# A hybrid SSD and GLA trunk on one core: the first gate stage's last sixteen moving pieces are split in their own tiles, some sums come sooner, and a pair of gate matmuls moves

## The chip, the cores and the metric

The kernel runs on one core of a Trainium2 chip. The metric is the device time of one execution in microseconds (us). Five engines work side by side and meet only at semaphores: TensorE (PE) multiplies, VectorE (DVE), ScalarE (ACT) and GpSimd (POOL) work element by element, and SyncE (SP) issues most of the DMA transfers; ACT issues the stores of results. Each engine takes its instructions in a fixed order, so that an instruction that waits holds everything behind it on its engine.

## What is computed

One layer over 2048 tokens and 16 meta tokens in front of them, width 1024, all in float32. Two branches, a Mamba-2 scan (SSD) and gated linear attention (GLA, 4 heads), read one combined projection; their results are projected, weighted by sigmoid gates, summed and projected out:

```python
u = rmsnorm(hres, norm_w)
proj = jnp.einsum('bld,dn->bln', u, w_in)
z, xbc, dt_raw, q, k, v, g_gla, a_lr, merge_g = split_cols(proj, IN_WIDTHS)
...
gate_logit = jnp.einsum('blr,rk->blk', a_lr, gla_gate_w2) + gla_gate_b
log_a = (jax.nn.log_sigmoid(gate_logit.astype(jnp.float32)) / GLA_GATE_TEMP)
...
o = rmsnorm(jnp.concatenate([o_m, o_r], axis=1), gla_norm_w)
y_gla = o.reshape(b, l, GLA_DV) * jax.nn.silu(g_gla)
branches = jnp.stack([y_ssd.astype(y_gla.dtype), y_gla], axis=2)
branch_proj = jnp.einsum('blnc,ncd->blnd', branches, w_branch)
gates = jax.nn.sigmoid(merge_g.reshape(b, l, N_BRANCH, D_MODEL))
merged = jnp.sum(gates * branch_proj, axis=2)
return hres + jnp.einsum('bld,de->ble', merged, w_out)
```

## The kernel before

Every float32 factor is held as a high and a low part, and a product is three matmuls: `accum` (L212) issues high by high (L214), high by low (L215) and low by high (L216). So each piece that is multiplied is first split: ACT copies it to the high part, which rounds it, and DVE subtracts that from the piece, which gives the low part (POOL does it for some weights, L190).

The program has two halves. The first, to about 1458 us, goes through four blocks of 512 tokens (the first with the 16 meta tokens). For each it projects `u` by the columns of `w_in` (L214 to L216 with "ue" and "whl"), runs the SSD scan (L600 to L702) and the GLA scan (around L925 to L980). The pieces are generators which `step` advances in turn; PE's and SP's order in this half is the order in which the code issues (`manual_schedule`). `gates` makes the decay of the GLA heads, two heads in one turn: per head a matmul pair by the small gate weights `w2` (L488, into a bank "pj" for the segment with the meta tokens and a bank "pt" for the rest), read by DVE (L490) and ACT (L491); after both heads exp and ln on ACT (L493, L494), and the running sums later. In block 0 this falls between the z projections, which write the same two "pj" banks, and the SSD step that has L664, L689, L690 and L692 on PE. The z halves have 48 matmuls each.

In the second half (`Stage`, L1088) seven large multiplications (gates 0, two branches, gates 1, two branches, out) are done by a scheme of seven products over 2 by 2 blocks. A stage goes through rows n of blocks; each row has products p in the order 1, 2, 6, 7, 5, 3, 4, for two rows in turn. Each product is 4 pieces times 3 matmuls, 24 for a pair of rows. `b` are the moving pieces, 4 for each p: for p=1, 2 the blocks themselves, for 7, 5, 4 and 6 sums that were stored before, for p=3 a block. `load_b` (SP, L1103) brings a piece into a buffer "br", and `prep_b` splits it into a tile `b` (ACT L1108, DVE L1109). `a` are the stationary pieces: `load_a` loads four blocks a11, a21, a22, a12 of a row ("ar", L1115), `sum_a` makes on POOL s1 = a21 + a22 (L1124), s2 = s1 - a11 (L1125), a11 - a21 in place (L1126) and s4 = a12 - s2 (L1127), and `prep_a` splits what a product uses (ACT L1133, DVE L1134): a11 for p=1, a12 for 2, s2 for 6, a11 - a21 for 7, s1 for 5, s4 for 3, a22 for 4. `snapshot` (ACT L1168) keeps a partial sum, `total` (DVE L1185) adds one, and the gates take a tanh (ACT L1192) and are stored (L1382).

The first products of gates 0 (p = 1, 2, 6 of rows 0 and 1) are put between the steps of block 3's last GLA head, by the table `between`. That head ends with a mean of squares over each token (`ssq`), its inverse root `rstd` (DVE L258, then a power on POOL, L259), the scaling of the output "ot" (ACT L969), eight transposes on PE (L976), a product with the gate (DVE L977) and the store of y (L980). From there on only SP's order is written out by a table `todo`: `at(pos, fn)` puts a call behind the product number `pos`. A scheduler orders the other engines by these calls. The last sixteen moving pieces of the first stage are those of p = 7, 5, 3 and 4.

```python
pos = begins[si] - 12 + 0.8 * q if si else {3: -0.5, 4: 5.5, 5: 6.5, 6: 8.5}[q // 4]
at(pos - (4 if si else 0.1), lambda st=st, p=p, j=j: st.load_b(p, j))
at(pos, lambda st=st, p=p, j=j: st.prep_b(p, j))
```

Of the kernel before, what the change touches and what calls it, by code (L numbers as in the profile page):

```python
# [15 lines left out]
P = 128  # L16
# [27 lines left out]
def trunk_kernel(ctx: ExitStack, tc: tile.TileContext, xm, xmt, w_feat, w_tok, w_v3, w_zm, w_br, w_o,  # L44
# [423 lines left out]
    def gates(o):  # L468
# [12 lines left out]
        for h2 in range(0, GH, 2):  # L481
            gmt = mk(wk, [P, 2, META + BLK], F32, "tok4", bufs=NT4)
            for h in (h2, h2 + 1):
                gm = gmt[:, h % 2, :tt]
                gb = gate_b[:, h:h + 1]
                for i, (a, n) in enumerate(o.segs_all):
                    ps = bank(*((pj, "pj") if m0 and i == 0 else (pt, "pt")))
                    nc.tensor.matmul(ps[:, :n], w2[:, h * P:(h + 1) * P], ast[:, a:a + n],  # L488
                                     start=True, stop=True)
                    nc.vector.tensor_scalar(gm[:, a:a + n], ps[:, :n], gb, 0.0, op0=ALU.add, op1=ALU.min)  # L490
                    evicted[:] = [nc.scalar.activation(g_all[:, h, a:a + n], ps[:, :n], AF.Abs, bias=gb)]  # L491
            ga = g_all[:, h2:h2 + 2, :tt]
            nc.scalar.activation(ga, ga, AF.Exp, scale=-1.0)  # L493
# [294 lines left out]
    def gla_scan(o, h, last=False):  # L788
# [165 lines left out]
        for c0 in range(0, NCH, 2):  # L954
# [11 lines left out]
            yield  # L966
        r = rstd_of(ssq, 4, 1.0 / 256)
        for c in range(NCH):
            nc.scalar.activation(ot[:, c], ot[:, c], AF.Identity, scale=r[:, c:c + 1])  # L969
        yield  # L970
# [54 lines left out]

    early_b = {}

# [60 lines left out]
    class Stage:  # L1088
# [8 lines left out]
        def load_b(self, p, j):  # L1097
            src = {1: lambda j: self.braw(j, 0), 2: lambda j: self.braw(4 + j, 0), 3: lambda j: self.braw(4 + j, 1),
                   4: lambda j: self.sums[1][j][:, 1], 5: lambda j: self.sums[0][j][:, 1],
                   6: lambda j: self.sums[1][j][:, 0], 7: lambda j: self.sums[0][j][:, 0]}[p]  # L1100
            pool, tag, nb = bt_raws["early" if "all" not in bt_raws or (4 * PS.index(p) + j) % 3 == 2 else "all"]
            raw = self.braws[p, j] = mk(pool, [P, BLK], F32, tag, bufs=nb)
            nc.sync.dma_start(raw, src(j))  # L1103

        def prep_b(self, p, j):
            raw = self.braws[p, j]
            t = u_tile(0)[:, :, :BLK] if p < 3 else mk(bpl[p], [P, 2, BLK], F32R, f"b{p}")
# [13 lines left out]
        def sum_a(self, n):  # L1121
# [6 lines left out]
            self.a[n].update({3: s4, 4: a22, 5: s1, 6: s2, 7: a21})  # L1128

        def prep_a(self, n, p):  # L1130
            src = self.a[n][p]
            t = mk(apl, [P, 2, 4, P], F32R, "a")
            nc.scalar.activation(t[:, 0], src, AF.Copy)  # L1133
            latest[:] = [nc.vector.tensor_tensor(t[:, 1], src, t[:, 0].bitcast(F32), op=ALU.subtract)]  # L1134
            self.a[n][p] = t
# [213 lines left out]
    for si, st in enumerate(stages):  # L1349
        for q in range(0 if si else 12, 28):  # L1350
            p, j = PS[q // 4], q % 4
            pos = begins[si] - 12 + 0.8 * q if si else {3: -0.5, 4: 5.5, 5: 6.5, 6: 8.5}[q // 4]
            at(pos - (4 if si else 0.1), lambda st=st, p=p, j=j: st.load_b(p, j))
            at(pos, lambda st=st, p=p, j=j: st.prep_b(p, j))
# [31 lines left out]
    st.b.update(early_b)  # L1386

    def b_ops(j):
        st.load_b(6, j)
        st.prep_b(6, j)  # L1390

    def early(n, p):
# [6 lines left out]
        1: [],  # L1399
        2: [lambda: st.prep_a(0, 1), lambda: st.prep_a(1, 1)],  # L1400
        3: [lambda: early(0, 1), lambda: st.prep_a(0, 2)],
        4: [lambda: st.sum_a(0), lambda: early(1, 1), lambda: st.prep_a(1, 2)],
        5: [lambda: early(0, 2), lambda: st.prep_b(6, 0), lambda: st.load_b(6, 2)],
        6: [lambda: early(1, 2), lambda: st.sum_a(1), lambda: st.prep_b(6, 1), lambda: st.load_b(6, 3)],
        7: [lambda: st.prep_a(0, 6), lambda: st.prep_b(6, 2)],
# [121 lines left out]
```

## Time and profile before

| | |
|---|---|
| median of 3 runs | 2242.24 us (2240.61 to 2245.01) |
| the profiled execution | 2246.45 us |
| its span, first to last instruction | 2244.7 us |
| mean granted clock of TensorE | 0.997 |
| PE idle, all | 32.8 us |
| of it, waits for low halves of moving pieces (L1109) | 3.9 us, 3 times |
| of it, wait of the gate matmul (L488) | 3.1 us, once |

The profile is of one execution. In a timeline each row has the start and the length in us, the engine, the line, the operation, the tile written and those read, how many alike stand together, and in brackets how long the engine sat idle before it and what ended that. Lengths of matmuls overlap, since they are pipelined: the distance between starts tells what one costs. In a table of windows the columns are the window, its length, the busy time of PE, PE's weight loads, DVE, ACT and POOL with the number of instructions, the granted clock of PE, the busy share of the DMA engines, and GB/s. A row of the waits has what waited for what, total, times and longest. A row of DMA issues has KB of each and the median time from issue to landing.

### The profile page before, as it was taken

The page shows a single profiled execution, that of the slowest core. Times are in us where ns is not written, and L with a number is a line of the kernel's source. Part 1 is how long each engine was busy: PE and PEld are TensorE (multiplying, and loading weights), DVE is VectorE, ACT ScalarE, POOL GpSimd, SP SyncE. Part 2 cuts the span into 40 slices and gives each one's busy share as a digit, 9 for nine tenths or more (in the row PEclk, how much of TensorE's full clock was granted, in tenths as well). Part 3 has the DMA queues.
Part 4 walks back from the last instruction along what each step waited for, and adds up shares of the span by engine and source line. Part 5 has one row for each costly group of instructions (what it writes and reads, how often), then busy time and mean ns, then how long its engine had stood idle before and what let it go on. Part 6 is the DMA issues. An engine that isn't in the chain of part 4 may idle for free.

```text
span 2244.7 us, 34971 instructions
## 1 busy us (share of the span) xinstructions
PE 2211.9 (99%) x11789; PEld 1896.8 (85%) x11789; DVE 1577.0 (70%) x2935; ACT 1187.0 (53%) x2767; POOL 693.9 (31%) x689
## 2 busy tenths in 40 slices
PE   7999999999999999999999999999999999999998
PEld 7999999888888888888988888878888888888887
DVE  5775676677557676567677666674679945789866
ACT  5666655575445456544465544454644545454544
POOL 5444433223212122221212100066233374324341
PEclk9999999999999999999999999999999999999999
DMA  9767875767777667778667664376768866787753
GB/s 313 247 222 234 273 259 202 237 209 240 240 244 260 212 213 237 241 245 272 207 212 233 213 211 160 127 250 198 241 227 289 303 221 217 237 282 245 261 177 121
DMA packets 313699, 517.95 MB, mean 231 GB/s; under 512 B 28080, under 2 KB 162480, under 8 KB 313520
## 3 DMA queue, kind: packets, MB, share of 16 engines
q1 hardware_dynamic: 247008, 419.89, 57.8%
q10 hardware_dynamic: 65872, 93.74, 11.5%
q8 instruction: 92, 1.51, 0.3%
q0 software_dynamic: 640, 2.10, 0.2%
q14 instruction: 87, 0.71, 0.1%
HBM read 368.42 MB, written 147.19 MB: 230 GB/s over the span
## 4 chain that ended last, share of the span: by engine, by line
PE 89%; DVE 4%; DMA 3%; ACT 2%; issue 1%; POOL 1%; SPq 0%; POOLq 0%; ACTq 0%; DVEq 0%
PE pj L214 20%; PE pj L216 20%; PE pj L215 19%; PE pt L215 4%; PE pt L214 4%; PE pt L216 4%; PE pc L689 2%; PE pc L214 2%; PE pc L216 2%; PE pc L215 2%; PE pc L850 2%; PE pc L690 1%; DMA acc<-in_xmt 1%; PE pc L692 1%; PE pc L958 1%
## 5 line engine op out<-in xcount | busy, mean ns | idle before, releaser
L214 PE MATMUL pj<-ue,whl 128*128 128x264 f32 (+1 forms) x672 | 235.3, 350 | 1.9 <-ACT acc L596 1.2
L216 PE MATMUL pj<-ue,whl 128*128 128x264 f32 (+1 forms) x672 | 229.7, 342 | 0.0
L215 PE MATMUL pj<-ue,whl 128*128 128x264 f32 (+1 forms) x672 | 228.8, 340 | 0.0
L214 PE MATMUL pj<-uo,whl 128*128 128x512 f32 x512 | 205.7, 402 | 0.0
L216 PE MATMUL pj<-uo,whl 128*128 128x512 f32 x512 | 200.1, 391 | 0.0
L215 PE MATMUL pj<-uo,whl 128*128 128x512 f32 x512 | 199.5, 390 | 0.0
L214 PE MATMUL pj<-b,a 128*128 128x512 f32 (+1 forms) x484 | 188.9, 391 | 0.7 <-DVE io L1252 0.5
L216 PE MATMUL pj<-b,a 128*128 128x512 f32 (+1 forms) x484 | 188.9, 390 | 0.3 <-DVE a L1134 0.3
L215 PE MATMUL pj<-b,a 128*128 128x512 f32 (+1 forms) x484 | 187.6, 388 | 0.0
L600 DVE SCALAR_TENSOR_TENSOR acc<-cin,hcw,acc 128x512 f32<-128x512 f32 (+1 forms) x192 | 156.7, 816 | 39.7 <-ACT acc L596 38.6
L83 POOL TENSOR_TENSOR wr<-wr 128x256 f32<-128x256 f32 x80 | 66.0, 826 | 371.8 <-DMA wr<-y 158.1
L1124 POOL TENSOR_TENSOR as<-ar,ar 128x512 f32<-128x512 f32 x40 | 62.9, 1572 | 374.7 <-DMA ar<-in_w_br 179.9
L1134 DVE TENSOR_TENSOR a<-ar,a 128x512 fp32r<-128x512 f32 x160 | 130.8, 824 | 65.0 <-ACT a L1133 63.5
L1109 DVE TENSOR_TENSOR b<-br,b 128x512 fp32r<-128x512 f32 x140 | 128.9, 943 | 18.1 <-ACT b L1108 17.8
L214 PEld LDWEIGHTS pj<-ue,whl 128*128 128x128 f32 x672 | 126.2, 188 | 17.7 <-ACT acc L596 1.7
L216 PEld LDWEIGHTS pj<-ue,whl 128*128 128x128 f32 x672 | 126.4, 188 | 14.9
L215 PEld LDWEIGHTS pj<-ue,whl 128*128 128x128 f32 x672 | 126.4, 188 | 14.7
L177 POOL TENSOR_TENSOR whl<-wr,whl 128x512 fp32r<-128x512 f32 (+1 forms) x76 | 96.9, 1282 | 126.2 <-ACT whl L175 94.4
L1168 ACT ACTIVATE sn<-pj 128x512 f32<-128x512 f32 x118 | 70.0, 593 | 123.8 <-PE pj L216 70.8
L1134 DVE TENSOR_TENSOR a<-as,a 128x512 fp32r<-128x512 f32 x120 | 101.6, 848 | 45.2 <-ACT a L1133 42.5
L1133 ACT ACTIVATE a<-ar 128x512 fp32r<-128x512 f32 x160 | 99.0, 624 | 64.7 <-PE pt L216 30.2
L215 PE MATMUL pt<-b,a 128*128 128x512 f32 x320 | 125.6, 392 | 3.9 <-DVE b L1109 3.9
(329 smaller groups left out, 6467.6 us busy)
## 6 DMA issues: line engine op xcount, KB each, us to landing
whl<-k_s SPq DMA_DIRECT2D x96, 512.0 KB, 3.7
whl<-k_g SPq DMA_DIRECT2D x96, 512.0 KB, 4.3
whl<-k_v SPq DMA_DIRECT2D x36, 512.0 KB, 4.0
wr<-in_w_feat SPq DMA_DIRECT2D x64, 256.0 KB, 4.5
k_s<-whl SPq DMA_DIRECT2D x32, 512.0 KB, 3.9
cb<-cumd SPq DMA_DIRECT2D x64, 256.0 KB, 5.1
y<-gg ACTq DMA_DIRECT2D x64, 256.0 KB, 4.2
k_g<-whl SPq DMA_DIRECT2D x32, 512.0 KB, 4.0
```

The costliest lines, as they stand in the source:

```text
L83: nc.gpsimd.tensor_tensor(o, x, y, op=ALU.subtract)
L177: nc.gpsimd.tensor_tensor(hl[:, 1], raw, hl[:, 0].bitcast(F32), op=ALU.subtract)
L214: nc.tensor.matmul(ps, sh, mh, start=first, stop=False, **kw)
L215: nc.tensor.matmul(ps, sh, ml, start=False, stop=False, **kw)
L216: nc.tensor.matmul(ps, sl, mh, start=False, stop=last, **kw)
L600: convd[:] = [nc.vector.scalar_tensor_tensor(acc, cin[:, k:k + tt], hcw[:, ti, k:k + 1], acc, op0=ALU.mult, op1=ALU.add)]
L689: nc.tensor.matmul(py[:, h * 64:(h + 1) * 64], dm[:, h], xdt[:, h], start=True, stop=True)
L1109: nc.vector.tensor_tensor(t[:, 1], raw, t[:, 0].bitcast(F32), op=ALU.subtract)
L1124: nc.gpsimd.tensor_tensor(s1, a21, a22, op=ALU.add)
L1133: nc.scalar.activation(t[:, 0], src, AF.Copy)
L1134: latest[:] = [nc.vector.tensor_tensor(t[:, 1], src, t[:, 0].bitcast(F32), op=ALU.subtract)]
L1168: nc.scalar.activation(sn, self.ps[n, "a"], AF.Copy)
```

## The change

In four parts. In block 0 `gates` yields once between the third and the fourth head. In the last head of the last block rstd is issued after the second sum (s2) of row 1, and the high part of p=6 of rows 0 and 1 is made after the scaling of "ot". `sum_a` of rows 0 and 1 is cut in three: s1 and s2 go into the table `between` at 2, in front of the first early products; a11 - a21 comes at -0.5 and s4 at 0 of the table `todo`. And the pieces of p = 7, 5, 3 and 4 of the first stage are loaded into the low half of their own tile instead of a buffer "br", then split there; those of 5, 3 and 4 are loaded 3 positions ahead instead of 0.1.

```diff
--- before.py
+++ after.py
@@ -489,6 +489,8 @@
                                      start=True, stop=True)
                     nc.vector.tensor_scalar(gm[:, a:a + n], ps[:, :n], gb, 0.0, op0=ALU.add, op1=ALU.min)
                     evicted[:] = [nc.scalar.activation(g_all[:, h, a:a + n], ps[:, :n], AF.Abs, bias=gb)]
+                if m0 and h == 2:
+                    yield
             ga = g_all[:, h2:h2 + 2, :tt]
             nc.scalar.activation(ga, ga, AF.Exp, scale=-1.0)
             nc.scalar.activation(ga, ga, AF.Ln, bias=1.0)
@@ -964,9 +966,10 @@
                 jk = mk(wk, [P, 256], BF16, "junk", bufs=1)
                 nc.scalar.activation(jk, ot[:, c], AF.Square, accum_out=ssq[:, c:c + 1])
             yield
-        r = rstd_of(ssq, 4, 1.0 / 256)
+        with tc.issue_after(summed[-1].ins) if o.b == nblk - 1 and h == GH - 1 and summed else nullcontext():
+            r = rstd_of(ssq, 4, 1.0 / 256)
         for c in range(NCH):
-            nc.scalar.activation(ot[:, c], ot[:, c], AF.Identity, scale=r[:, c:c + 1])
+            scaled[:] = [nc.scalar.activation(ot[:, c], ot[:, c], AF.Identity, scale=r[:, c:c + 1])]
         yield
         if o.b == nblk - 1 and h == GH - 1:
             yield
@@ -1023,7 +1026,7 @@
                 yield next(pieces)
         assert next(pieces, pieces) is pieces
 
-    early_b = {}
+    early_b, summed, scaled = {}, [], []
 
     def first_b():
         loaded = []
@@ -1098,11 +1101,20 @@
             src = {1: lambda j: self.braw(j, 0), 2: lambda j: self.braw(4 + j, 0), 3: lambda j: self.braw(4 + j, 1),
                    4: lambda j: self.sums[1][j][:, 1], 5: lambda j: self.sums[0][j][:, 1],
                    6: lambda j: self.sums[1][j][:, 0], 7: lambda j: self.sums[0][j][:, 0]}[p]
+            if p in (7, 5, 3, 4) and self is stages[0]:
+                t = self.b[p, j] = mk(bpl[p], [P, 2, BLK], F32R, f"b{p}")
+                nc.sync.dma_start(t[:, 1].bitcast(F32), src(j))
+                return
             pool, tag, nb = bt_raws["early" if "all" not in bt_raws or (4 * PS.index(p) + j) % 3 == 2 else "all"]
             raw = self.braws[p, j] = mk(pool, [P, BLK], F32, tag, bufs=nb)
             nc.sync.dma_start(raw, src(j))
 
         def prep_b(self, p, j):
+            if (p, j) in self.b:
+                t = self.b[p, j]
+                nc.scalar.activation(t[:, 0], t[:, 1].bitcast(F32), AF.Copy)
+                nc.vector.tensor_tensor(t[:, 1], t[:, 1].bitcast(F32), t[:, 0].bitcast(F32), op=ALU.subtract)
+                return
             raw = self.braws[p, j]
             t = u_tile(0)[:, :, :BLK] if p < 3 else mk(bpl[p], [P, 2, BLK], F32R, f"b{p}")
             nc.scalar.activation(t[:, 0], raw, AF.Copy)
@@ -1127,10 +1139,29 @@
             nc.gpsimd.tensor_tensor(s4, a12, s2, op=ALU.subtract)
             self.a[n].update({3: s4, 4: a22, 5: s1, 6: s2, 7: a21})
 
+        def sum_first(self, n):
+            a11, a21, a22, a12 = self.araws[n]
+            s1, s2 = [mk(rpl, [P, 4, P], F32, "as", bufs=NAS) for _ in range(2)]
+            nc.gpsimd.tensor_tensor(s1, a21, a22, op=ALU.add)
+            summed[:] = [nc.gpsimd.tensor_tensor(s2, s1, a11, op=ALU.subtract)]
+            self.a[n].update({4: a22, 5: s1, 6: s2})
+
+        def sum_second(self, n):
+            a11, a21, a22, a12 = self.araws[n]
+            nc.gpsimd.tensor_tensor(a21, a11, a21, op=ALU.subtract)
+            self.a[n][7] = a21
+
+        def sum_third(self, n, s2):
+            a12 = self.araws.pop(n)[3]
+            s4 = mk(rpl, [P, 4, P], F32, "as", bufs=NAS)
+            nc.gpsimd.tensor_tensor(s4, a12, s2, op=ALU.subtract)
+            self.a[n][3] = s4
+
         def prep_a(self, n, p):
             src = self.a[n][p]
             t = mk(apl, [P, 2, 4, P], F32R, "a")
-            nc.scalar.activation(t[:, 0], src, AF.Copy)
+            with tc.issue_after(scaled[-1].ins) if n < 2 and p == 6 and self is stages[0] else nullcontext():
+                nc.scalar.activation(t[:, 0], src, AF.Copy)
             latest[:] = [nc.vector.tensor_tensor(t[:, 1], src, t[:, 0].bitcast(F32), op=ALU.subtract)]
             self.a[n][p] = t
 
@@ -1350,7 +1381,7 @@
         for q in range(0 if si else 12, 28):
             p, j = PS[q // 4], q % 4
             pos = begins[si] - 12 + 0.8 * q if si else {3: -0.5, 4: 5.5, 5: 6.5, 6: 8.5}[q // 4]
-            at(pos - (4 if si else 0.1), lambda st=st, p=p, j=j: st.load_b(p, j))
+            at(pos - (4 if si else 0.1 if q < 16 else 3), lambda st=st, p=p, j=j: st.load_b(p, j))
             at(pos, lambda st=st, p=p, j=j: st.prep_b(p, j))
     for i, (st, n, p) in enumerate(order):
         if i >= NEARLY:
@@ -1385,6 +1416,16 @@
     st = stages[0]
     st.b.update(early_b)
 
+    second = {}
+
+    def first_sums(n):
+        st.sum_first(n)
+        second[n] = st.a[n][6]
+
+    for n in range(2):
+        at(-0.5, lambda n=n: st.sum_second(n))
+        at(0, lambda n=n: st.sum_third(n, second[n]))
+
     def b_ops(j):
         st.load_b(6, j)
         st.prep_b(6, j)
@@ -1397,11 +1438,11 @@
     between = {
         0: [lambda: st.load_a(0), lambda: st.load_a(1), lambda: st.load_b(6, 0), lambda: st.load_b(6, 1)],
         1: [],
-        2: [lambda: st.prep_a(0, 1), lambda: st.prep_a(1, 1)],
+        2: [lambda: st.prep_a(0, 1), lambda: st.prep_a(1, 1), lambda: first_sums(0), lambda: first_sums(1)],
         3: [lambda: early(0, 1), lambda: st.prep_a(0, 2)],
-        4: [lambda: st.sum_a(0), lambda: early(1, 1), lambda: st.prep_a(1, 2)],
+        4: [lambda: early(1, 1), lambda: st.prep_a(1, 2)],
         5: [lambda: early(0, 2), lambda: st.prep_b(6, 0), lambda: st.load_b(6, 2)],
-        6: [lambda: early(1, 2), lambda: st.sum_a(1), lambda: st.prep_b(6, 1), lambda: st.load_b(6, 3)],
+        6: [lambda: early(1, 2), lambda: st.prep_b(6, 1), lambda: st.load_b(6, 3)],
         7: [lambda: st.prep_a(0, 6), lambda: st.prep_b(6, 2)],
         8: [lambda: st.prep_b(6, 3), lambda: early(0, 6), lambda: st.prep_a(1, 6)],
         9: [lambda: early(1, 6)],
```

The lines behind the additions have higher numbers in the new kernel: L664, L689, L690 and L692 become L666, L691, L692 and L694, L1103 becomes L1106 or L1110, L1109 becomes L1116 (in place) or L1121, L1115 becomes L1127, L1124 to L1127 become L1136 and so on, and L1145, L1146, L1151 and L1157 for rows 0 and 1, L1134 becomes L1165 and L1185 becomes L1216. The orders differ in two places only.

On PE, in block 0, before (`act` behind L488 is the low-rank gate input, `w` its weights; `pj` from L214 on is a z half):

```order
L488 MATMUL pj_1550<-act_1005,w_387 128x264
L488 MATMUL pt_1554<-act_1005,w_387 128x264
L488 MATMUL pj_1558<-act_1005,w_387 128x264
L488 MATMUL pt_1562<-act_1005,w_387 128x264
L664 MATMUL pt_1568<-cst,act_682 128x128
L664 MATMUL pt_1568<-cst,act_772 128x128
L664 MATMUL pt_1568<-cst,act_858 128x128
L689 MATMUL pc_1588<-c_179_1440,sq_1447 128x64 x4
L690 MATMUL pc_1588<-s_ssd,act_936 128x256
L692 MATMUL pc_1594<-c_180_1442,bt_1445 128x256
L214 MATMUL pj_1603<-whl_1605,ue_313 128x256
```

And in the changed kernel, first there, then at the end of that z half:

```order
L488 MATMUL pj_1550<-act_1005,w_387 128x264
L488 MATMUL pt_1554<-act_1005,w_387 128x264
L666 MATMUL pt_1558<-cst,act_682 128x128
L666 MATMUL pt_1558<-cst,act_772 128x128
L666 MATMUL pt_1558<-cst,act_858 128x128
L691 MATMUL pc_1578<-c_179_1440,sq_1447 128x64 x4
L692 MATMUL pc_1578<-s_ssd,act_936 128x256
L694 MATMUL pc_1584<-c_180_1442,bt_1445 128x256
L214 MATMUL pj_1593<-whl_1595,ue_313 128x256
```

```order
L216 MATMUL pj_1594<-whl_1601,ue_337 128x256
L488 MATMUL pj_1655<-act_1005,w_387 128x264
L488 MATMUL pt_1659<-act_1005,w_387 128x264
L691 MATMUL pc_1667<-c_200_1562,sq_1569 128x64 x4
L692 MATMUL pc_1667<-s_ssd,act_936 128x256
L694 MATMUL pc_1673<-c_201_1564,bt_1567 128x256
```

The pair of the fourth head has moved behind the 48 matmuls of the z half; L666 to L694 now stand directly behind the pair of the third.

On POOL, at the end of the last GLA head, before (`as` are s1, s2 and s4, `ar` the loaded blocks):

```order
L259 TENSOR_TENSOR rstd_16657<-rstd_16657,mhalf 128x4
L1124 TENSOR_TENSOR as_16682<-ar_16591,ar_16593 128x512
L1125 TENSOR_TENSOR as_16683<-as_16682,ar_16589 128x512
L1126 TENSOR_TENSOR ar_16591<-ar_16589,ar_16591 128x512
L1127 TENSOR_TENSOR as_16684<-ar_16595,as_16683 128x512
L1124 TENSOR_TENSOR as_16758<-ar_16599,ar_16601 128x512
L1125 TENSOR_TENSOR as_16759<-as_16758,ar_16597 128x512
L1126 TENSOR_TENSOR ar_16599<-ar_16597,ar_16599 128x512
L1127 TENSOR_TENSOR as_16760<-ar_16603,as_16759 128x512
```

And in the changed kernel:

```order
L1145 TENSOR_TENSOR as_16657<-ar_16591,ar_16593 128x512
L1146 TENSOR_TENSOR as_16658<-as_16657,ar_16589 128x512
L1151 TENSOR_TENSOR ar_16591<-ar_16589,ar_16591 128x512
L1145 TENSOR_TENSOR as_16661<-ar_16599,ar_16601 128x512
L1146 TENSOR_TENSOR as_16662<-as_16661,ar_16597 128x512
L259 TENSOR_TENSOR rstd_16665<-rstd_16665,mhalf 128x4
L1151 TENSOR_TENSOR ar_16599<-ar_16597,ar_16599 128x512
L1157 TENSOR_TENSOR as_16859<-ar_16595,as_16658 128x512
L1157 TENSOR_TENSOR as_16861<-ar_16603,as_16662 128x512
```

Both pairs of s1 and s2 now stand in front of rstd, and the a11 - a21 of row 1 and both s4 behind it.

On DVE, around the low halves of b7, before (`br` behind L1109 is a loaded piece, `b` its split tile; `a` behind L1134 the split stationary pieces):

```order
L1134 TENSOR_TENSOR a_16861<-as_16682,a_16861 128x512
L1109 TENSOR_TENSOR b_3077_16843<-br_16835,b_3077_16843 128x512
L1134 TENSOR_TENSOR a_16864<-as_16758,a_16864 128x512
L1109 TENSOR_TENSOR b_3078_16846<-br_16837,b_3078_16846 128x512
L1134 TENSOR_TENSOR a_16867<-as_16684,a_16867 128x512
L1109 TENSOR_TENSOR b_3079_16849<-br_3075_16839,b_3079_16849 128x512
L1109 TENSOR_TENSOR b_3080_16852<-br_16841,b_3080_16852 128x512
L1134 TENSOR_TENSOR a_16911<-as_16760,a_16911 128x512
```

And in the changed kernel:

```order
L1165 TENSOR_TENSOR a_16853<-as_16657,a_16853 128x512
L1216 TENSOR_TENSOR as_16703<-as_16703,pc_16743 128x512
L1165 TENSOR_TENSOR a_16856<-as_16661,a_16856 128x512
L1116 TENSOR_TENSOR b_3071_16829<-b_3071_16829 128x512
L1116 TENSOR_TENSOR b_3072_16831<-b_3072_16831 128x512
L1116 TENSOR_TENSOR b_3073_16833<-b_3073_16833 128x512
L1116 TENSOR_TENSOR b_3074_16835<-b_3074_16835 128x512
L1165 TENSOR_TENSOR a_16863<-as_16859,a_16863 128x512
L1116 TENSOR_TENSOR b_3082_16866<-b_3082_16866 128x512
L1116 TENSOR_TENSOR b_3083_16868<-b_3083_16868 128x512
```

Before, a low half of a stationary piece stands between every two of b7's first three, and they come behind the s1 of both rows; now the four stand together, behind the totals of rows 0 and 1 (L1216). On SP the order from there is p = 7, 5 and 3, four loads each, then the four "ar" of row 2, then p = 4, and ACT makes the high halves in the order of DVE's lows.

## Prediction

> **What bounds the kernel now.** I read the page first: shares of busy time, then the chain of waits.
>
> ```profile
> span 2244.7 us, 34971 instructions
> PE 2211.9 (99%) x11789; PEld 1896.8 (85%) x11789; DVE 1577.0 (70%) x2935; ACT 1187.0 (53%) x2767; POOL 693.9 (31%) x689
> PE 89%; DVE 4%; DMA 3%; ACT 2%; issue 1%; POOL 1%; SPq 0%; POOLq 0%; ACTq 0%; DVEq 0%
> ```
>
> TensorE (PE) sets the time, and no matmul is removed. What a new order can win is PE's idle time, 2244.7 - 2211.9 = 32.8 us, and any stretch in which PE runs at a lower clock. Next I asked for whom PE waits:
>
> ```profile
> PE pt L215 <- DVE b L1109: 3.9, 3, 1.7
> PE pj L488 <- ACT acc L596: 3.1, 1, 3.1
> PE pj L216 <- DVE a L1134: 0.3, 1, 0.3
> ```
>
> The columns are total, times and longest, in us. These three lie where the diff works: L488 in block 0's gates (place A), the other two at the start of the first gate stage (place B). Windows of both places, with PE's busy time second and its granted clock under PEclk (1.00 is full):
>
> ```profile
> 103.16:106.57 3.41, 1.28 (x9) 0.92 (x8) 3.41 (x8) 1.24 (x4) 0.00 (x0) 1.00 0.63 206
> 106.58:113.38 6.80, 5.80 (x22) 5.21 (x23) 6.62 (x14) 6.80 (x19) 4.09 (x4) 0.50 0.52 170
> 1478.80:1482.20 3.40, 1.67 (x7) 1.05 (x6) 3.40 (x4) 2.34 (x5) 3.40 (x3) 1.00 0.59 195
> 1476.00:1487.00 11.00, 7.11 (x30) 4.89 (x29) 11.00 (x11) 6.10 (x12) 7.04 (x5) 1.00 0.58 189
> ```
>
> At A the clock falls to half while PE waits, and stays there for 6.80 us, in which PE is busy for 5.80. At full clock that work needs 2.90, so the wait costs its 3.15 us and 2.90 more. At B, PE idles 3.89 us of 11 without losing clock.
>
> **Place A: the second L488 pair of block 0 goes behind a z half.** PE, with ACT, DVE and POOL beside it, before:
>
> ```profile
> 104.16 0.28 PE L488 MATMUL pt<-act,w 48*128 48x264 f32 x1
> 107.58 0.58 PE L488 MATMUL pj<-act,w 48*128 48x264 f32 x1 [3.15 <-ACT acc L596]
> 112.07 0.78 PE L214 MATMUL pj<-whl,ue 128*128 128x256 f32 x1
> 118.56 1.00 PE L689 MATMUL pc<-c,sq 128*128 128x64 f32 x8
> 106.97 0.56 ACT L596 ACTIVATE acc<-pj,hcb,hcw 128x264 f32<-128x264 f32 x1
> 105.76 0.68 DVE L680 TENSOR_TENSOR sq<-sq,sq 128x512 f32<-128x512 f32 x1
> 106.87 1.65 POOL L190 TENSOR_TENSOR whl<-wr,whl 128x512 fp32r<-128x512 f32 x1 [5.99 <-ACT whl L189]
> 108.93 1.27 POOL L190 TENSOR_TENSOR whl<-wr,whl 128x512 fp32r<-128x512 f32 x1 [0.28 <-DVE tok L490]
> ```
>
> The pair needs a bank of "pj" that ACT's L596 lets go at 107.53; all of PE's program stands behind it. In the new order L664 x3, L689, L690 and L692 come first, and the same group one step earlier, at full clock, gives their length:
>
> ```profile
> 95.93 0.49 PE L664 MATMUL pt<-cst,act 128*128 128x128 f32 x3
> 96.25 1.00 PE L689 MATMUL pc<-c,sq 128*128 128x64 f32 x8
> 97.83 0.47 PE L214 MATMUL pj<-ue,whl 128*128 128x264 f32 x1
> ```
>
> So PE frees at 104.44, does L664 until 104.9, and then waits after all: L689 reads what DVE's L680 finishes at 106.44. From there 97.83 - 96.25 = 1.58 us bring it to 108.0, past 107.53, so the z half gets its bank. That half needs the low part of its weights from POOL, ready at 108.52 and 110.20: I take 0.4 and 1.0 us of new gaps. The half itself takes 118.56 - 112.07 = 6.49 us before, of which 113.38 - 112.07 = 1.31 at half clock: 5.84 at full. It ends at 108.0 + 0.4 + 1.0 + 5.84 = 115.2. The moved pair, 0.23 each by the starts of the matmuls, adds 0.5: 115.8 at the place that was reached at 118.56. **Gain 2.8 us.**
>
> Idle time hardly changes (1.5 + 0.4 + 1.0 against 3.15); the gain is the clock. In 103.16:106.57 PE was busy 1.28 of 3.41 (38%) and the clock fell; in 1478.80:1482.20 it was busy 1.67 of 3.40 (49%) and the clock stayed. The new gap leaves PE busy some 1.8 of the worst 3.41 (53%), on the good side of both. What the move delays, exp and ln of the gates and their sums, is used a step later. Ends: 0, if the clock falls all the same, and 6.0, if all that the stall costs goes.
>
> [...]
>
> **Place B, what it removes.** PE, DVE and POOL around the p=7 products:
>
> ```profile
> 1464.32 0.48 PE L214 MATMUL pc<-ue,a 128*128 128x512 f32 x1
> 1469.96 0.39 PE L214 MATMUL pj<-b,a 128*128 128x512 f32 x1
> 1476.08 0.62 PE L214 MATMUL pt<-b,a 128*128 128x512 f32 x2
> 1480.54 0.50 PE L215 MATMUL pt<-b,a 128*128 128x512 f32 x1 [1.73 <-DVE b L1109]
> 1486.30 0.62 PE L214 MATMUL pj<-b,a 128*128 128x512 f32 x2
> 1478.73 1.75 DVE L1109 TENSOR_TENSOR b<-br,b 128x512 fp32r<-128x512 f32 x1
> 1484.98 1.88 DVE L1109 TENSOR_TENSOR b<-br,b 128x512 fp32r<-128x512 f32 x3
> 1478.34 1.59 POOL L1125 TENSOR_TENSOR as<-as,ar 128x512 f32<-128x512 f32 x1
> ```
>
> 24 matmuls take 1469.96 - 1464.32 = 5.64 us for p=2, and 1486.30 - 1476.08 = 10.22 for p=7: 4.6 lost, since each low half of b7 needs 1.75 us on DVE beside a POOL sum (0.63 alone, 1.88 / 3), and a low half of "a" stands between every two. In the new order the four b7 lows stand together, ahead of them s1 and s2 are long done, and their loads are queued sooner. The loads wait until the last head's transposes let go of the memory (1465), take 4.7 to 6.4 us, and are split by some 1476, when p=7 starts: **4.6 gained**. p=6 took 1476.08 - 1469.96 = 6.12, 0.48 over p=2; its 0.3 wait for a low half of s2 goes too: **0.5 gained**. Splitting in place has the same two instructions of the same size; I price it at nothing, hidden behind PE's 5.64 us per pair of products (uncovered, 0.62 on ACT and 0.63 on DVE for a piece). On SP the n=2 loads of "a" now go behind twelve b loads; that too is nothing, since n=2's first products start only after n=0 and 1 are done, at 1499.
>
> **Place B, what it adds.** rstd, which the last head's transposes need, stands on POOL behind both s1/s2 pairs:
>
> ```profile
> 1450.06 3.40 SPq L1115 DMA_DIRECT2D ar<-in_w_feat  x7
> 1457.51 1.15 ACT L1133 ACTIVATE a<-ar 128x512 fp32r<-128x512 f32 x2 [1.48 <-DMA ar<-in_w_feat]
> 1460.98 1.01 POOL L259 TENSOR_TENSOR rstd<-rstd,mhalf 128x4 f32<-128x4 f32 x1 [13.67 <-DVE rstd L258]
> 1462.05 1.70 ACT L969 ACTIVATE ot<-ot,rstd 128x256 f32<-128x256 f32 x4
> br<-gate_t SPq DMA_DIRECT2D x10, 256.0 KB, 4.7
> y<-gg ACTq DMA_DIRECT2D x4, 256.0 KB, 5.7
> ```
>
> POOL is idle for 13.67 us ahead of rstd, so three of the four sums fit. The last pair needs the last but one of the seven loads, which lands about 1458.5 (the first of that piece's four at 1457.5); with 1.3 and 1.6 us for the two sums, it is done at 1461.5. Then rstd ends at 1462.5 instead of 1461.99; ACT has a second b6 piece (0.62) ahead of L969 too. I take **0.75 us lost** at the transposes; ends 0 and 2.5 (a landing as late as the slowest, with a DVE operation beside each sum).
>
> Sums of n=2 and the rest of n=0, 1 now lie beside the b5, b3 and b4 lows. p=7, 5, 3 and 4 would run from 1476 to 1499; DVE has 12 lows and some 8 of "a" there, 13 us alone and 1.1 more for each that meets a POOL sum. Eight sums may meet them: 21 of 22 us. b5's second load also waits on SP for a y store (5.7 us to land). I take **1.6 us of new waits**; ends 0 and 4.6 (all that p=7 lost).
>
> [...]
>
> **Sum.** A 2.8 + B (4.6 + 0.5 - 0.75 - 1.6 = 2.75) = 5.55 us. The profiled run took 2246.45 us (span 2244.7), which would become 2240.9; it lies 4.2 above the median of the three times, 2242.24, from which I subtract the same: **2236.7 us**.
>
> **Rivals.**
> 1. *B is given back later.* The p=7 waits come again at p=3 or p=4: 4.6 of new waits instead of 1.6, 2239.7. For it: DVE full through 1476 to 1487; against: PE waited nowhere for b5, b3 or b4 lows before, in the same 22 us of PE work.
> 2. *The clock didn't fall at A in the executions that are timed*, or falls in both kernels: A gives 0, 2239.5. For it: the three times differ by 4.4 us, more than the 2.9 that a fall costs. [...]
> 3. *Slower: SP's queue starves p=5 and p=3.* SP issues in order, and a load that waits for a store's landing holds all behind it: b5[1] for a y store, which ACT issues only behind the last b6 pieces. If that store goes out at 1471.5 and lands 5.7 later, b5[1] lands at 1481.9 to 1483.6; its split adds 0.6 and 1.75: 1486 against 1482.5, a wait of 3.5 us; a second like it for b3[2] behind a g store (4.0), and the clock at half for 2.9 behind such waits, with 2.0 more at the transposes. 12.4 lost against 7.9 gained: 2246.7. It decides once new waits pass 7.9.
>
> **Chances.** Forecast 0.50 (own range 2233 to 2238.5), rival 1 0.20, rival 2 0.16, rival 3 0.14. 0.2% is 4.5 us, about what a measurement of this kernel tells from no change: faster is below 2237.8, slower above 2246.7. Of the forecast 0.42 lies below 2237.8 and of rivals 1 and 2 0.08: faster 0.50. Same: 0.08 + 0.28 = 0.36. Slower: 0.14. The range goes from 2232 (both gains, no new wait at B and none of the lost 0.75) to 2245 (short of rival 3).
>
> **What would show it.** A: no fall of the granted clock near 106 us, L689 waiting about 1.5 for L680, and the place of 118.56 reached about 115.8. B: p=7 in under 6 us, no wait for b7 lows, rstd near 1461.5 with L976 later by under 1 us relative to the p=1 products; small waits at p=5 to p=4. I am wrong if PE waits over 2 us for the transposes, if a b5 or b3 load lands after its product has begun, or if the clock at A is half in both traces or in neither.

## The result and the profile after

The changed kernel takes 2236.34 us (median of 10 runs, 2233.94 to 2240.27) against 2242.09 us before (10 runs, 2240.21 to 2245.01): a ratio of 0.9973, with a 95% interval of 0.9965 to 0.998. That is 5.8 us faster. The profiled executions differ by more, 2244.7 - 2236.0 = 8.7 us of span.

The page after, span and busy times, and then the longer waits of TensorE (total, times, longest):

```profile
span 2236.0 us, 34965 instructions
PE 2209.7 (99%) x11789; PEld 1896.8 (85%) x11789; DVE 1568.4 (70%) x2935; ACT 1187.0 (53%) x2767; POOL 689.2 (31%) x689
```

```profile
PE pc L691 <- DVE sq L682: 2.0, 2, 1.6
PE pc L214 <- DVE c L948: 1.3, 3, 0.6
PE pt L979 <- ACT ot L972: 0.4, 1, 0.4
```

PE's busy time fell by 2.2 us with the same 11789 matmuls. By the windows before and after, 5.80 / 2 - 3.41 / 2 = 1.2 us of that is time at half clock that went; the other 1.0 isn't explained. The rest of the 8.7 us, 32.8 - 26.3 = 6.5, is idle time. The waits for low halves of moving pieces (3.9) and for L596 (3.1) are gone; new are a wait of 1.6 for the low part of sq at place A and 0.4 at the transposes.

Place A, from the timeline of PE after the change, and then windows with its clock (busy time of PE second, granted clock third from the end):

```profile
103.20 0.28 PE L488 MATMUL pt<-act,w 48*128 48x264 f32 x1
105.51 1.10 PE L691 MATMUL pc<-c,sq 128*128 128x64 f32 x8 [1.56 <-DVE sq L682]
114.75 0.39 PE L488 MATMUL pj<-act,w 48*128 48x264 f32 x1
115.18 1.10 PE L691 MATMUL pc<-c,sq 128*128 128x64 f32 x8
```

```profile
103.38:106.80 3.42, 1.86 (x14) 1.58 (x14) 3.42 (x9) 2.25 (x7) 0.91 (x1) 1.00 0.26 94
106.80:110.21 3.41, 3.41 (x15) 3.14 (x14) 3.41 (x8) 3.41 (x13) 3.14 (x4) 0.50 0.42 143
110.21:113.62 3.41, 3.41 (x31) 3.41 (x30) 3.41 (x8) 1.32 (x4) 0.05 (x1) 1.00 1.03 292
```

From the third head's second L488 to the SSD step behind the z half it is 115.18 - 103.20 = 11.98 us, against 118.56 - 104.16 = 14.40: 2.4 gained. The wait for sq is there, and the clock falls all the same, but for 3.41 us instead of the 6.83 of before (table below).

Place B, the starts of the products on PE, then POOL and DVE:

```profile
1453.93 0.40 PE L214 MATMUL pj<-ue,a 128*128 128x512 f32 x1
1460.02 1.97 PE L979 MATMUL pt<-cst,ot 128*128 128x128 f32 x8 [0.36 <-ACT ot L972]
1461.74 0.47 PE L214 MATMUL pc<-ue,a 128*128 128x512 f32 x1
1467.38 0.39 PE L214 MATMUL pj<-b,a 128*128 128x512 f32 x1
1472.87 0.63 PE L214 MATMUL pt<-b,a 128*128 128x512 f32 x2
1478.38 0.39 PE L214 MATMUL pj<-b,a 128*128 128x512 f32 x1
```

```profile
1454.52 1.72 POOL L1145 TENSOR_TENSOR as<-ar,ar 128x512 f32<-128x512 f32 x1
1456.31 1.62 POOL L1146 TENSOR_TENSOR as<-as,ar 128x512 f32<-128x512 f32 x1
1458.04 1.39 POOL L259 TENSOR_TENSOR rstd<-rstd,mhalf 128x4 f32<-128x4 f32 x1
1480.02 1.60 POOL L1136 TENSOR_TENSOR as<-ar,ar 128x512 f32<-128x512 f32 x1 [8.54 <-DMA ar<-in_w_feat]
```

```profile
1453.69 3.09 DVE L1165 TENSOR_TENSOR a<-ar,a 128x512 fp32r<-128x512 f32 x2 [0.18 <-ACT a L1164]
1456.70 1.26 DVE L258 TENSOR_SCALAR rstd<-ssq 128x4 f32<-128x4 f32 x1
1469.65 3.58 DVE L1116 TENSOR_TENSOR b<-b 128x512 fp32r<-128x512 f32 x4
```

p=1 starts at 1453.93, p=2 at 1461.74, p=6, 7 and 5 at 1467.38, 1472.87 and 1478.38. p=7 takes 5.51 us where it took 10.22, p=6 5.49 where it took 6.12. From p=1 to p=2, with the transposes between, it is 7.81 us; before it was 1464.32 - 1457.71 = 6.61. POOL's sums of row 2 start at 1480.02, 8.5 us after the last sum ahead of them, since their loads now stand behind twelve others; the four low halves of b7 end at 1473.2, long before.

### The profile page after: what moved, and what is told of

Read it like the earlier page. It is cut to its first block, busy times and chain, and to the rows that moved or that the text cites. A ratio compares the mean times of both kernels' runs of the same rounds, so it can differ in the third digit from the quotient of the medians.

```text
span 2236.0 us, 34965 instructions
## 1 busy us (share of the span) xinstructions
PE 2209.7 (99%) x11789; PEld 1896.8 (85%) x11789; DVE 1568.4 (70%) x2935; ACT 1187.0 (53%) x2767; POOL 689.2 (31%) x689
## 4 chain that ended last, share of the span: by engine, by line
PE 72%; DMA 1%; DVE 1%; ACT 1%; POOL 0%; issue 0%; POOLq 0%; SPq 0%; ACTq 0%; DVEq 0%
PE pj L214 15%; PE pj L216 15%; PE pj L215 15%; PE pt L214 4%; PE pt L215 4%; PE pt L216 4%; PE pc L216 2%; PE pc L214 2%; PE pc L215 2%; PE pc L691 2%; PE pc L852 1%; PE pc L692 1%; PE pc L960 1%; PE pc L694 1%; PE pt L666 1%; DMA acc<-in_xmt 1%
## 5 line engine op out<-in xcount | busy, mean ns | idle before, releaser
L214 PE MATMUL pj<-ue,whl 128*128 128x264 f32 (+1 forms) x672 | 235.4, 350 | 1.2 <-ACT acc L598 1.2
L214 PE MATMUL pj<-uo,whl 128*128 128x512 f32 x512 | 205.8, 402 | 0.0
L214 PE MATMUL pj<-b,a 128*128 128x512 f32 (+1 forms) x484 | 189.0, 391 | 0.5 <-DVE io L1283 0.5
L1165 DVE TENSOR_TENSOR a<-ar,a 128x512 fp32r<-128x512 f32 x160 | 136.0, 858 | 61.3 <-ACT a L1164 60.5
L1136 POOL TENSOR_TENSOR as<-ar,ar 128x512 f32<-128x512 f32 x38 | 60.8, 1600 | 371.7 <-DMA ar<-in_w_br 185.9
L214 PEld LDWEIGHTS pj<-ue,whl 128*128 128x128 f32 x672 | 126.4, 188 | 16.7 <-ACT acc L598 1.6
L1165 DVE TENSOR_TENSOR a<-as,a 128x512 fp32r<-128x512 f32 x120 | 100.6, 840 | 45.0 <-ACT a L1164 42.0
L214 PE MATMUL pt<-b,a 128*128 128x512 f32 x320 | 125.7, 393 | 0.0
L215 PE MATMUL pt<-b,a 128*128 128x512 f32 x320 | 125.3, 392 | 0.0
```

The lines of the kernel that those rows point to most:

```text
L214: nc.tensor.matmul(ps, sh, mh, start=first, stop=False, **kw)
L215: nc.tensor.matmul(ps, sh, ml, start=False, stop=False, **kw)
L1136: nc.gpsimd.tensor_tensor(s1, a21, a22, op=ALU.add)
```

## The experiments

Times, each beside runs of the kernel before on the same chip (its medians were 2243.27, 2242.4 and 2243.13 us for the three groups), and four lengths from each profile: the stretch at A from the SSD step ahead of the gates to the one behind the z half (the starts of the first and third L689, or L691, behind 94 us); how long the clock was at half there; from the start of p=1 to that of p=2; and from the start of p=1 to the end of the span.

| kernel | median us | ratio (95%) | A | half clock | p=1 to 2 | p=1 to end |
|---|---|---|---|---|---|---|
| before | 2242.09 | | 22.31 | 6.83 | 6.61 | 787.0 |
| changed | 2236.34 | 0.9973 (0.9965 to 0.998) | 19.88 | 3.41 | 7.81 | 782.1 |
| a_alone | 2239.4 | 0.9991 (0.9983 to 1.0) | 18.31 | 0 | 6.35 | 785.1 |
| b_alone | 2239.52 | 0.9986 (0.9977 to 0.9995) | 22.77 | 6.83 | 7.69 | 781.9 |
| sums_alone | 2240.89 | 0.9987 (0.9979 to 0.9996) | 22.75 | 6.83 | 7.70 | 782.8 |
| loads_alone | 2240.51 | 0.9988 (0.9979 to 0.9997) | 22.45 | 6.83 | 6.35 | 784.1 |
| late_loads | 2238.61 | 0.9981 (0.9973 to 0.999) | 19.91 | 3.41 | 7.94 | 782.7 |
| before_hold | 2242.17 | 0.9996 (0.9987 to 1.0004) | 22.64 | 6.83 | 6.66 | 784.4 |
| before_fill | 2244.14 | 1.0005 (0.9996 to 1.0014) | 21.33 | 0 | 6.35 | 785.9 |
| after_fill | 2237.33 | 0.9973 (0.9961 to 0.9984) | 18.32 | 0 | 7.91 | 782.1 |
| after_fill48 | 2239.68, one run | | 18.31 | 0 | 7.92 | 782.2 |
| rstd_mid | 2235.57 | 0.9967 (0.9954 to 0.9979) | 19.93 | 3.41 | 6.33 | 781.3 |
| mid_fill | 2235.21 | 0.9969 (0.9958 to 0.9981) | 18.32 | 0 | 6.75 | 781.6 |
| after_again | 2237.76 | 0.9976 (0.9967 to 0.9985) | 18.32 | 0 | 7.72 | 783.1 |

Single runs of one kernel scatter by 4 to 8 us (where there are ten or more), so the times settle only what is worth 2 us or more; smaller steps are read from the profiles.

### Each place alone

`a_alone` is the kernel before with the yield:

```diff
+                if m0 and h == 2:
+                    yield
```

> The kernel before with the one yield in block 0's gates alone. Theory (place A is worth 2.4 us by the two traces, through a shorter stretch at half clock): 2239.7 us, PE 12.0 us from the third head's second L488 to the second L689 instead of 14.4, p=7 still about 10.2 us long. Rival (the offset is an accident of where the clock's window met the wait): within 1 us of before, 2242. If the new wait for the low part of sq (1.5 us) is there, the clock is at half for one window of 3.4 us or for none.

`b_alone` is the changed kernel without it.

> The changed kernel without the yield. Theory (the places add up): the wait of 3.1 us at L488 and its half clock are back, p=7 stays at 5.5 us without a wait, 2236.3 + 2.4 = 2238.7 us. Rival (A is worth nothing in the timed runs, B all): 2236.5.

The places are worth about the same, 0.0009 and 0.0014 of the time (2.0 and 3.1 us by the ratios), and they add up: 5.1 against the 6.1 of the whole. The times alone don't refute the rival that A is worth nothing: the interval of `a_alone` reaches 1.0, and that of `b_alone` overlaps that of the whole change. The profiles speak against it: the stretch at A takes 18.31 to 19.93 us in all five that have the yield and no spare matmuls, and 22.31 to 22.77 in all five that have neither. In `a_alone` the clock didn't fall at all, so that the 12.0 us expected from the third head's second L488 to the second L691 became 10.4; in `b_alone` it fell for 6.83 us as before.

In `a_alone`, place B has the order of the kernel before, and yet p=7 took 5.51 us without a wait, where 10.2 was expected. It met POOL in another way:

```profile
1465.10 1.75 POOL L1128 TENSOR_TENSOR ar<-ar,ar 128x512 f32<-128x512 f32 x1
1472.11 1.50 POOL L1129 TENSOR_TENSOR as<-ar,as 128x512 f32<-128x512 f32 x1 [5.26 <-DMA g<-as]
```

```profile
1475.36 0.62 PE L214 MATMUL pj<-b,a 128*128 128x512 f32 x2
1477.60 0.50 PE L215 MATMUL pj<-b,a 128*128 128x512 f32 x1 [1.62 <-DVE b L1111]
```

s4 writes a buffer that a store of g still read; here POOL stood still for 5.26 us until that store had landed (1.66 in the profile before), and the first two low halves of b7 went through in 0.68 us each in that time. POOL's sums then met the b5 lows, and PE waited 1.62 at p=5. So the 3.9 us at p=7 in the profile before were one outcome of several for the same order; the second half of `a_alone` (785.1) and of `before_fill` (785.9) is 1 to 2 us shorter than in that profile (787.0), without a change there.

### The parts of place B

`sums_alone` is the changed kernel without the yield, with `load_b`, `prep_b` and the load positions of before:

```diff
-            if p in (7, 5, 3, 4) and self is stages[0]:
-                t = self.b[p, j] = mk(bpl[p], [P, 2, BLK], F32R, f"b{p}")
-                nc.sync.dma_start(t[:, 1].bitcast(F32), src(j))
-                return
...
-            at(pos - (4 if si else 0.1 if q < 16 else 3), lambda st=st, p=p, j=j: st.load_b(p, j))
+            at(pos - (4 if si else 0.1), lambda st=st, p=p, j=j: st.load_b(p, j))
```

> The kernel before with s1 and s2 in front, rstd behind them and the p=6 pieces behind the scaling; no yield, pieces still loaded into shared buffers. Theory S (p=7 waited because its low halves met POOL sums and stood between low halves of a): p=7 loses its waits here already, 3 to 4 us gained, 2238.5. Theory L (the shared buffers let the pieces of b7 come too late): p=7 keeps waits of 3 us or more, and the transposes are 1.2 us later, so 2241.5 to 2243.

`loads_alone` is the kernel before with these lines of the change and with `prep_b` in place, and nothing else of it.

> The kernel before with the sixteen pieces loaded into their own tiles, three positions sooner, and split in place; sums, rstd and the gates as before. Theory S: DVE's order around b7 is nearly as before and POOL's sums lie where they did, so p=7 still takes 9 to 10 us, 2241 to 2242. Theory L: p=7 in under 7 us, 2238.5.

Both work, and they overlap: each alone takes some 2.8 us off the time, together 3.1 (`b_alone`). The second half shortens to 782.8 with the sums and to 784.1 with the loads, from 785.1 to 787.0. For the sums that is theory S in its mechanism, though the time, 2240.89, isn't the 2238.5 it gave. For the loads theory S missed: p=7 lost its waits there too (0.28 is left), with DVE's order around b7 nearly the old one. POOL in `loads_alone` shows why:

```profile
1472.60 1.81 POOL L1136 TENSOR_TENSOR as<-ar,as 128x512 f32<-128x512 f32 x1 [2.30 <-ACT a L1142]
1482.23 2.91 POOL L1133 TENSOR_TENSOR as<-ar,ar 128x512 f32<-128x512 f32 x1 [7.82 <-DVE b L1113]
```

POOL does nothing from 1474.4 to 1482.2: the loads of row 2 stand behind those of b5 and b3, so that row 2's sums cannot meet the low halves of b7. (The row names DVE as what ended the pause; in the changed kernel, with the same order of loads, it is the DMA of "ar", after 8.54 us.) Before, the sums ran from 1476.74 to 1483.3, through most of p=7. `before_hold` does that to the kernel before, with one term in the table of positions, which moves the call of row 2's sums two positions back along with its loads:

```diff
-            pos = i - LOAD + (n % 2)
+            pos = i - LOAD + (n % 2) + (2 if i == 14 else 0)
```

> The kernel before with one edit: the four loads of row 2's stationary blocks go behind the loads of b5 and b3 on SP, so that POOL's sums of row 2 cannot run beside the low halves of b7. Sums in front, tiles and gates as before. Theory Q (what the sooner loads do at p=7 is to hold back POOL's sums of row 2): p=7 takes under 7 us though DVE's order around b7 is the old one, second half 1.5 to 2.5 us shorter, 2240 to 2241. Rival (the low halves of a between those of b7, and s4, are enough for the waits): p=7 stays at 9 to 10 us, 2242 to 2243.

DVE in `before_hold`, then PE:

```profile
1472.46 1.78 DVE L1109 TENSOR_TENSOR b<-br,b 128x512 fp32r<-128x512 f32 x1
1474.17 0.68 DVE L1134 TENSOR_TENSOR a<-as,a 128x512 fp32r<-128x512 f32 x1
1474.77 0.68 DVE L1109 TENSOR_TENSOR b<-br,b 128x512 fp32r<-128x512 f32 x1
1475.38 0.68 DVE L1134 TENSOR_TENSOR a<-as,a 128x512 fp32r<-128x512 f32 x1
1475.98 2.48 DVE L1109 TENSOR_TENSOR b<-br,b 128x512 fp32r<-128x512 f32 x4
```

```profile
1474.30 0.50 PE L215 MATMUL pt<-b,a 128*128 128x512 f32 x1 [0.49 <-DVE b L1109]
1497.11 0.51 PE L215 MATMUL pt<-b,a 128*128 128x512 f32 x1 [0.90 <-DVE b L1109]
```

The order of the lows is that of before, but for two b5 lows that come ahead of the last "a". The first low of b7 takes 1.78 us, beside s4 of row 1 on POOL; the others and the "a" between them take 0.6 to 0.7 each, and p=7 takes 5.35 us with a wait of 0.49. So POOL's sums beside b7's lows caused the waits at p=7, and the low halves of "a" between them alone do not; so far theory Q holds. The second half is 784.4, 0.7 to 2.6 shorter than with the old order, with new waits of 0.90 and 0.16 in it, since the sums now meet the b4 lows. In the time nothing shows: 2242.17 is not the 2240 to 2241 expected and isn't told from before.

`late_loads` is the changed kernel with the second position of before:

```diff
-            at(pos - (4 if si else 0.1 if q < 16 else 3), lambda st=st, p=p, j=j: st.load_b(p, j))
+            at(pos - (4 if si else 0.1), lambda st=st, p=p, j=j: st.load_b(p, j))
```

> The changed kernel with the pieces of p=5, 3 and 4 loaded 0.1 positions ahead as before, still into their own tiles. Theory (the gain at B is the order on POOL and DVE, loads are not on the path): no wait at p=5, 3 or 4 over 0.5 us, 2236 to 2237. Rival (the sooner loads carry it): waits of 1 to 3 us for low halves of b5, b3 or b4, 2238 to 2239.5.

No wait came at p=5, 3 or 4, and the second half is 782.7 against 781.9 to 783.1 with the sooner loads. The median, 2238.61, lies where the rival put it, but without the waits that the rival needs, and its interval (0.9973 to 0.999) overlaps that of the change (0.9965 to 0.998). By the profile the sooner loads are worth half a microsecond at most beside the sums; by the times this stays open.

### rstd behind one pair of sums

`rstd_mid` puts only the first pair of s1 and s2 in front of rstd:

```diff
-        2: [lambda: st.prep_a(0, 1), lambda: st.prep_a(1, 1), lambda: first_sums(0), lambda: first_sums(1)],
+        2: [lambda: st.prep_a(0, 1), lambda: st.prep_a(1, 1), lambda: first_sums(0)],
...
-        4: [lambda: early(1, 1), lambda: st.prep_a(1, 2)],
+        4: [lambda: early(1, 1), lambda: st.prep_a(1, 2), lambda: first_sums(1)],
```

> The changed kernel with rstd behind the first pair of s1 and s2 only: the second pair is issued after it. Theory (the transposes come 1.2 us later since rstd waits on POOL for the second pair, and on DVE for low halves slowed by it): p=2 starts 6.6 to 7.2 us after p=1 instead of 7.8, p=7 still without a wait over 0.5 us, 2235.5. Rival (the second pair, now later, meets DVE's low halves of p=6 and p=7): a wait of 1 us or more comes back at p=6, p=7 or p=5, 2236 to 2238.

POOL and PE in `rstd_mid`:

```profile
1455.36 1.01 POOL L259 TENSOR_TENSOR rstd<-rstd,mhalf 128x4 f32<-128x4 f32 x1 [1.74 <-DVE rstd L258]
1456.35 1.30 POOL L1145 TENSOR_TENSOR as<-ar,ar 128x512 f32<-128x512 f32 x1
```

```profile
1453.12 0.39 PE L214 MATMUL pj<-ue,a 128*128 128x512 f32 x1
1458.66 1.04 PE L979 MATMUL pt<-cst,ot 128*128 128x128 f32 x8
1459.45 0.48 PE L214 MATMUL pc<-ue,a 128*128 128x512 f32 x1
```

rstd starts 2.24 us after p=1 instead of 4.11, the transposes take 1.04 instead of 1.97, and p=2 follows p=1 by 6.33 us, less than the 6.6 expected at the least: the 1.2 us that the change lost, and 0.3 more, are back. No wait over 0.3 us came at p=6, 7 or 5. The second half is 781.3, the shortest of all, 0.6 to 1.8 below the five profiles that have the whole of the change at B (781.9 to 783.1). The time, 2235.57, has an interval (0.9954 to 0.9979) that overlaps that of the change.

### The clock at place A

`after_fill` puts twelve matmuls by operands that are at hand into the bank that the third head's second L488 then overwrites; `before_fill` puts 24 there in the kernel before, and `after_fill48` repeats L488 itself twelve times:

```diff
+                    if m0 and h == 2 and i:
+                        for _ in range(12):
+                            nc.tensor.matmul(ps[:, :n], o.u[0][:, 0, :P], o.u[0][:, 0, a:a + n], start=True, stop=True)
```

> The changed kernel with twelve spare matmuls of 264 columns (all 128 rows, result overwritten) in front of the third head's second L488, about 1.4 us of work in the place of the 1.56 us wait for the low part of sq. Theory (what is left of place A is the fall of the clock behind an idle TensorE, which comes in some executions and not in others): clock at full all through, 11 us or less from that L488's old place to the next z half's end, and 0.5 to 1.7 us faster than the changed kernel, 2235. Rival (the fall has another cause than idle time): a stretch at half clock stays and the time is that of the changed kernel, 2236.3, or 1 us more.

> The kernel before with 24 such spare matmuls (2.9 us of work) in the place of the 3.15 us wait at the fourth head's L488; order and everything else as before. Theory (the wait costs more by the clock than by its length): no fall of the clock, 2.9 us faster than before, 2239.5 to 2240.5. Rival (the order of the move counts, not the clock): within 1 us of before.

> The changed kernel with twelve spare matmuls at the same place that use 48 rows of the array instead of 128 (the third head's own L488 repeated). One look at the clock. If any busy TensorE keeps the clock: full all through, as with the twelve of 128 rows. If few rows count for less: a window at half clock though TensorE is busy without a pause. Times within 2235 to 2238 either way.

The clock stayed at full in all three. With the change the stretch then takes 18.3 us, 1.6 less than where the clock fell for 3.41 us (19.88 to 19.93), and as long as in `a_alone` and `after_again` (below), where it didn't fall without spare matmuls either. The profiles differ in where the stretch lies behind the rise of the clock near 20 us (at 21.46 in the profile after, where matmuls of 288 columns start 0.24 us apart ahead of it and 0.13 behind it). Its first L691 starts 73.84, 74.33 and 74.36 us behind that rise in the three profiles with a fall, and 75.40 and 75.43 in the two without. `after_fill` (73.85) and `mid_fill` (74.22, below) lie where it fell, so by these two profiles the twelve spare matmuls of 128 rows kept the clock there. `after_fill48` (75.68) lies beside the two in which it didn't fall, so it doesn't show whether matmuls of 48 rows would keep it where it fell.

In the time of `after_fill`, 2237.33 instead of 2235, nothing of the 1.6 shows; it is less than the width of the interval. `before_fill` was no gain in time: 2244.14 where 2239.5 to 2240.5 was expected. Its stretch is 21.33, only 1.2 below the mean of the old order, since the spare matmuls, 3.19 us of them, hold the gate's own result back, DVE's work goes on behind it, and 1.59 of wait for sq is new one step later. Here what the wait costs by the clock was not won by work that delays others. (The stretch of `before_fill` begins 75.43 us behind the rise, where none of the five of the old order lies, so that it isn't shown that the spare matmuls kept its clock.)

`mid_fill` has both, twelve spare matmuls and rstd in the middle.

> rstd behind the first pair of sums and the twelve spare matmuls at place A together, on top of the change. Theory (both are what is left at the two places): clock at full all through the first half, p=2 6.3 us after p=1, 2233.5 to 2235. Rival (either is given back later, as the spare matmuls alone were not seen in the time): 2235.5 to 2237.

2235.21 us, 0.9969 (0.9958 to 0.9981): the lowest median of all, 1.1 below the change, but it isn't told from the change, nor from `rstd_mid`, and lies between the two ranges expected. By the profile it has the shorter stretch at A (18.32) and 781.6 at B; p=2 comes 6.75 us after p=1 instead of 6.3.

`after_again` is the changed kernel itself in the third group.

> The changed kernel once more, beside the others on the same chip. Theory: 2236 to 2237; the clock falls for one window of 3.4 us at place A or for none (three profiles of four that have the yield and no spare matmuls showed one). p=7 under 6 us. If a second window or a wait at p=7 shows, the reading of either place is wrong.

It took 2237.76 us, a ratio of 0.9976, over the 2236 to 2237 expected by 0.8. In its profile the clock did not fall, and p=7 took 5.51 us without a wait. So of five profiles that have the yield and no spare matmuls three show 3.41 us at half clock (changed, rstd_mid, late_loads), two none; all five without either show 6.83. The 3.42 us up to the point 85.33 us behind the rise of the clock, in which the wait for sq lay, first for `rstd_mid` and `late_loads`, where the clock fell at that point, then for `a_alone` and `after_again`, where it didn't:

```profile
101.79:105.21 3.42, 1.86 (x14) 1.36 (x12) 3.42 (x8) 1.71 (x5) 0.38 (x1) 1.00 0.40 131
```

```profile
102.81:106.23 3.42, 1.86 (x14) 1.39 (x13) 3.42 (x8) 1.74 (x5) 0.41 (x1) 1.00 0.37 128
```

```profile
102.81:106.23 3.42, 2.17 (x16) 1.65 (x14) 3.42 (x8) 1.25 (x4) 0.00 (x0) 1.00 0.85 288
```

```profile
101.32:104.74 3.42, 2.16 (x16) 1.64 (x14) 3.42 (x8) 1.25 (x5) 0.00 (x0) 1.00 0.88 291
```

In the first two PE was busy for 1.86 us of 3.42 (54%), and the granted clock was 0.50 in the 3.41 us behind; in the last two it was busy for 2.16 or 2.17 (63%), and the clock stayed at 1.00. The wait is 1.56 or 1.57 us each time; in the first two it lies wholly inside the row, in the last two about 0.3 of it comes behind.

## Why the prediction was right, and where it wasn't

The time came within 0.4 us of the 2236.7 predicted, the sign and the likeliest case held, and none of the rivals came true as a whole. But one of the prediction's own signs of being wrong did come: at A the clock is at half in both traces. The terms:

- *A, 2.8 us.* In the first profile 2.4; over five profiles with the yield (19.88, 19.93, 19.91, 18.31, 18.32) and five without (22.31, 22.77, 22.75, 22.45, 22.64) the mean is 3.3. The wait of 1.5 for sq was there (1.56). The step that failed is "the new gap leaves PE busy some 1.8 of the worst 3.41 (53%), on the good side of both": at 54% the clock fell, in three of five profiles, while at B it stayed at 48% (last section). That the number came out is luck, for two misses cancel: the 1.6 us that a fall of 3.41 us cost was not priced, and the 0.4 and 1.0 of new gaps for the low part of the z weights didn't come; between L694 and the next L488 the profile after has no wait of PE. Without a fall the move gains 22.58 - 18.31 = 4.3 (mean of the old order against `a_alone`); with it some 2.7, since the fall then lasts 3.41 us instead of 6.83. Rival 2 in its first half, that the clock doesn't fall before, is refuted by the five profiles in which it fell each time; its second half, that it falls in both kernels, came true in three of five, but A didn't give 0 there.
- *B, p=7's waits, 4.6.* 10.22 - 5.51 = 4.7 between these two profiles. But the old order loses 1 to 2 us less in other executions, as `a_alone` and `before_fill` show. The reason given had two halves; POOL's sums of row 2 were the one that mattered, as `before_hold` shows, and the low halves of "a" between alone were not.
- *On SP, "that too is nothing".* The place of row 2's loads behind the b loads was priced at nothing. It is right that no product waits for them; but it is this that keeps the sums of row 2 off b7's lows in `loads_alone`.
- *p=6, 0.5.* 6.12 - 5.49 = 0.6.
- *The transposes, -0.75.* Measured 7.81 - 6.61 = 1.2, inside the ends of 0 and 2.5, by another cause: no load was late (s1 of row 1 began at 1454.52 with no wait). rstd stood behind s2 until 1457.9, and its own DVE step ended at 1457.96, since the two low halves ahead of it, beside POOL's sums, took 3.09 us instead of 1.29, and the step itself 1.26 instead of 0.17. `rstd_mid` won it back.
- *New waits at p=5 to 4, -1.6.* This is the term of B that was mis-sized: none came. DVE's b4 lows did meet POOL (three took 5.20 us), but 5.51 us of PE work per pair of products hid it. From p=5 to the end the changed kernel was even 0.8 shorter (758.4 to 757.6); 0.23 of that is a wait for ACT (L1168) that only the profile before has there, and the rest stays unexplained. The end of 0 was the right one, and rival 1 and the slower rival fall with it.

The sum at B is 4.7 + 0.6 - 1.2 + 0.8 = 4.9 us between the two profiles, against 2.75 predicted. Against all profiles with the old order (787.0, 785.1, 785.9, mean 786.0) and with the whole change (782.1, 781.9, 782.1, 782.2, 783.1, mean 782.3) it is 3.7. Together with A's 3.3 that is 7.0, near the upper part of what the times show (0.9965 to 0.998: 4.5 to 7.8 us). So the total was met more closely (5.55 forecast, 5.8 measured) than the two places that it is added up from. Of the 8.7 us between the two profiled spans, 2.4 lie at A and 4.9 at B; 0.95 came ahead of A (96.25 against 95.30) and 0.4 between the places, where nothing was changed.

## What to carry to other kernels

A wait of the bounding engine can cost about as much again by what it does to the clock (here 3.15 us and 2.9, or 1.56 and 1.6). So shortening it can win more than its length: 1.6 us less of wait won 2.7 to 4.3 here. The same shorter wait still cost clock in three of five profiles and not in the other two, with the stretch 73.84 to 74.36 us behind the clock's rise in the three and 75.40 and 75.43 in the two, which this program doesn't choose. When an element-wise operation on one engine takes 1.75 us in one place and 0.68 in another, look at what the other engine does in that time before moving the operation itself; here moving four loads in a queue took most of the waits at p=7 away without a new order of the splits, though the second half stayed 2 us longer than with the whole change. And one profile is one outcome: the same order of work lost 3.9 us at one place or 1.6 at another, depending on when a store landed.

## What the hardware did that I had not expected

At A the granted clock fell 85.33 or 85.34 us behind its rise near 20 us in seven of the eight profiles that show a fall there, and 88.75 us behind it in the eighth (`sums_alone`). It stayed at half for 3.41 or 6.83 us. PE's busy share alone doesn't tell where it fell: at A 54% busy came before a fall, while at B 48% did not; that row is from the profile before:

```profile
1478.85:1482.26 3.41, 1.65 (x6) 1.05 (x6) 3.41 (x3) 2.29 (x4) 3.41 (x3) 1.00 0.61 195
```

B's matmuls there have 512 columns each; at A they are small and many. The columns of the moving operand (264 in "48x264") of all matmuls that start in the row are 3072 at B; at A they are 1360 to 1408 in the three rows with 54% busy, and 3024 and 3288 in the two with 63%. No run here changes the columns alone, so whether they have to do with the clock isn't shown.
